# Gate slices of layer 1 loaded and stored four token tiles at a time, in place, in buffers shared with the residual

## The chip, the cores and the metric

The kernel runs on one core of a Trainium2 chip. The core has five engines with instruction streams of their own: TensorE (PE, matrix products into PSUM), VectorE (DVE), ScalarE (ACT), GpSimd (POOL) and SyncE (SP), which in this kernel issues all DMAs. The metric is the device time of one execution in microseconds; three runs of the kernel before took 1652.52, 1655.86 and 1656.51 us, a median of 1655.86.

## What is computed

Two layers over 1024 tokens of width 1024, 16 heads of 64. Layer 1 is attention with a forget gate ("fox"), layer 2 dilated sliding windows in three groups. In each, the mixer's output is multiplied by a gate and projected back onto the residual:

```python
def fox_mixer(h, w_in, b_f, q_g, k_g):
    proj = h @ w_in
    q = rms_norm(proj[..., :INNER]...)      # k, v alike
    gate = proj[..., 3 * INNER:4 * INNER]
    c = jnp.cumsum(jax.nn.log_sigmoid(f_logit), axis=1)
    o = fox_attention(q, k, v, c)           # causal softmax(q k / 8 + c_q - c_k) v
    return o.reshape(B, S, INNER), gate

x = x + (o * jax.nn.silu(gate)) @ w_out     # in each layer
```

## The kernel before

Everything is tiled by 128 tokens (8 token tiles) and by head pairs (8 pairs of 2 heads, 128 columns). A matrix product in full precision is made of three products of half-precision parts (xh, xl: high and low part of the activations; w: both parts of a weight).

Stages, in order: the gates of layer 1 (`gates`, L885 on: a projection, then silu on ACT and DVE, stored as `gs_d` in DRAM); the attention of layer 1, head pair by head pair; the output projection of layer 1 (`project_t` with `grown`, which adds the residual tile `xr`); the gates of layer 2; the attention of layer 2; the last output projection (`project_t` with `finished`, again with residual tiles `xr`).

In layer 1's attention each head pair projects queries, keys and values of one token tile after the other (`project`, L694). `heads_pair` splits queries and keys into halves `hl` and a DMA transpose brings them into `qk_t` (L843); `qs` is a copy on DVE with the halves swapped (L850). For each of the eight query tiles `fox_tile` then takes a number of steps: `score` computes the scores on PE (L870), adds the forget bias `bc` (read from `c_d` by L1088; POOL adds the mask, L1122) and takes the minimum on DVE (L1125); `p_transpose` makes the exponentials on ACT, splits them into halves `ph` (ACT and POOL, L916 and L919), and a DMA transpose on SP makes `ptt` (L920); `values` multiplies with the values on PE (L927 to L929); `finish` divides by the sum, multiplies with the gate slice and writes `y` (L1155, L1158).

The gate slice of one token tile and one head pair (128 x 128, 64 KB) is loaded in `score` (L1106) into a buffer with the tag `gsl` (3 buffers in layer 1). `finish` writes y to a tile of its own (tag `y`, 2 buffers) and stores it to `y_d` (L1162); head pair 7 does not store it, but transposes it on PE at once (`turn_last`, L729). While pair 7 runs, `turn_y` reads the stored y of the other pairs back from `y_d` (`yt`, L1178) and transposes them on PE, as input of the output projection.

The residual tiles `xr` of both output projections, the gate tiles `ge` and two small constants use the tag `n2k` (2 KB per partition) with `cfg["nb"]` buffers, 3 of them.

What the functions issue is only a list. Each step is queued for a slot of a clock (`flow`) that ticks with the projection's products. At the end `order_engines` builds a graph of all instructions (which data each needs, which buffers must come free) and `plan_engines` plays it through with a duration for each instruction: an engine takes the ready instruction whose latest start is earliest. The order found is fixed for each engine. So a change of buffers or DMAs moves instructions on every engine, as far as times in this plan shift. DMAs are all issued by SP in the planned order.

Of the kernel before, what the change touches and what calls it, by code (L numbers as in the profile page):

```python
# [11 lines left out]
F32 = mybir.dt.float32  # L12
# [5 lines left out]
ALU = mybir.AluOpType  # L18
# [4 lines left out]
P = 128  # L23
# [5 lines left out]
HD = 64  # L29
NHP = NH // 2  # L30
# [407 lines left out]
def trunk(ctx, tc, ins, out, cfg):  # L438
    nc = tc.nc
# [7 lines left out]
    def pool(name, bufs, space=None):  # L447
        kw = {} if space is None else dict(space=space)
        return book.pool(ctx.enter_context(tc.tile_pool(name=name, bufs=bufs, **kw)), name, bufs, space)
# [3 lines left out]
    sb = pool("sb", 2)  # L453
# [16 lines left out]
    def lay(shape, dtype, name, tag):  # L470
        return layer["pool"].tile(shape, dtype, name=name, tag=tag, bufs=layer["bufs"][tag])
# [3 lines left out]
    y_d = dram.tile([S, D], F32, name="y_d")  # L475
# [6 lines left out]
    gs_d = dram.tile([S, D], F32, name="gs_d")  # L482
# [372 lines left out]
    def key_runs(look):  # L855

        runs = []
        for j in look:
            if runs and j % 2 and runs[-1][0] == j - 1:
                runs[-1][1] = 2  # L860
            else:
                runs.append([j, 1])
        return runs
# [106 lines left out]
    def column_factor(t):  # L970

        sq = lay([P, D], F32, name="xsq", tag="ptt")
        nb = ps_s.tile([P, 512], F32, name="nb", tag="s")
        for h in range(2):
            nc.scalar.activation(sq[:, 512 * h : 512 * (h + 1)], xts[t, h], AF.Square)
            for k in range(4 * h, 4 * h + 4):
                nc.tensor.matmul(nb[:, :P], ones.bitcast(F32), sq[:, k * P : (k + 1) * P], start=(k == 0), stop=(k == KT - 1))
        a, y = (nb[:, i * P : (i + 1) * P] for i in (2, 3))
        r = sm.tile([P, P], F32, name="dg", tag="dg", bufs=2)
        c = sm.tile([P, P], F32, name="cf", tag="dg", bufs=2)  # L980
        nc.vector.tensor_scalar(c, nb[:, :P], 1.0 / D, EPS, ALU.mult, ALU.add)
        nc.scalar.activation(r, c, AF.Ln)
        nc.scalar.activation(r, r, AF.Exp, scale=-0.5)
        nc.scalar.activation(a, r, AF.Square)
        nc.vector.scalar_tensor_tensor(a, a, -0.5, c, ALU.mult, ALU.mult)
        nc.vector.scalar_tensor_tensor(y, a, 1.5, r, ALU.add, ALU.mult)
        return y
# [26 lines left out]
    with book.early(nc, cfg["rush"]):  # L1014
        gain_scale(0, gt)
        nb = column_factor(0)
# [5 lines left out]
    with book.early(nc, cfg["rush"] / 2):  # L1022
        nb = column_factor(1)
# [49 lines left out]
    def urgent(fn, key, slot):  # L1073
        def go():
            if cfg[key]:
                with tc.high_priority(cfg[key]):
                    fn()
            else:
                fn()

        flow.at(slot, go)
# [3 lines left out]
    def load_bc(hp, h, es=(0, 1)):  # L1085
        for e in es:
            bcs[hp, e, h] = lay([P, 5 * P], F32, name="bc", tag="ga")
            nc.sync.dma_start(bcs[hp, e, h][:, P:], c_d[2 * hp + e, h * 512 : (h + 1) * 512].partition_broadcast(P))  # L1088

    def fox_tile(hp, t, kts, vt, sl):  # L1090
        LP = cfg["lpf"]
        nk = (t + 1) * P
        st = {}
        pieces = [(a, min(a + 512, nk)) for a in range(0, nk, 512)]
        both = len(pieces) == 1
        a0 = pieces[-1][0] // P
        placed = [*range(a0), t, *range(a0, t)]
        accs = {}
        ptl = {}
        ps = {0: [], 1: []}  # L1100

        def score(e, c):
            a, b = pieces[c]
            if e == 0 and c == 0:
                gs = st["gs"] = lay([P, P], F32, name="gsf", tag="gsl")
                nc.sync.dma_start(gs, gs_d[t * P : (t + 1) * P, hp * P : (hp + 1) * P])  # L1106
            if c == 0:
                accs[e] = BIG
                st["acc"] = sm.tile([P, 2], F32, name="acc", tag="acc", bufs=8)
            if t < 2:  # L1110
                if e == 0:
                    st["p"] = lay([P, 2, nk], F32, name="p", tag="p")
                p = st["p"][:, e]
            else:
                p = lay([P, b - a], F32, name="p", tag="p")
            ps[e].append(p)
            s = ps_s.tile([P, 512], F32, name="s", tag="s")
            bc = bcs[hp, e, a // 512]
            look = key_runs(range(a // P, b // P))
            if b == nk:  # L1120
                look = [[t, 1]] + key_runs(range(a // P, t))
                nc.gpsimd.tensor_add(bc[:, :P], bc[:, b - a : b - a + P], tri)  # L1122
            scores(s, kts[t // 2], t % 2, e, [(kts[j // 2], j % 2, n) for j, n in look])
            acc = st["acc"][:, c : c + 1]
            nc.vector.tensor_tensor_reduce(p, s[:, : b - a], bc[:, : b - a] if b == nk else bc[:, P:], -1.0, accs[e], ALU.add, ALU.min, acc)  # L1125
            accs[e] = acc
            pl = (cfg["pl"] & 1, cfg["pl"] >> 1 & 1)
            if c < len(pieces) - 1 or both and e == 0:
                return
            if both:  # L1130
                exps = [(ps[i][0], accs[i]) for i in range(2)]
                if t < 2:
                    splits = [(slice(0, 2), slice(0, nk), st["p"], pl[1])]
                else:
                    splits = [(i, slice(0, nk), ps[i][0], pl[i]) for i in range(2)]
                pt = p_transpose(2, nk, exps, splits)
                for i in range(2):
                    ptl[i] = [(pt[:, i, 0, k], pt[:, i, 1, k], j) for k, j in enumerate(placed)]
            else:
                exps = [(p, accs[e]) for p in ps[e]]  # L1140
                splits = [(0, slice(*pieces[i]), ps[e][i], pl[i]) for i in range(2)]
                pt = p_transpose(1, nk, exps, splits)
                ptl[e] = [(pt[:, 0, 0, k], pt[:, 0, 1, k], j) for k, j in enumerate(placed)]

        def values(e):
            if e == 0:
                st["o"] = ps_o.tile([P, 2, HD + 1], F32, name="o", tag="o")
            pv(st["o"], e, ptl[e], vt)
            if e == 1:
                finish()  # L1150

        def finish():
            o = st["o"]
            rec = sm.tile([P, 2], F32, name="rec", tag="rec")
            nc.vector.reciprocal(rec, o[:, :, HD])  # L1155
            y = sb.tile([P, P], F32, name="y", tag="y")
            for e in range(2):
                nc.vector.scalar_tensor_tensor(y[:, e * HD : (e + 1) * HD], o[:, e, :HD], rec[:, e : e + 1], st["gs"][:, e * HD : (e + 1) * HD], ALU.mult, ALU.mult)  # L1158
            if hp == NHP - 1:
                turn_last(y, t, flow.now + 3, 0)  # L1160
            else:
                nc.sync.dma_start(y_d[t * P : (t + 1) * P, hp * P : (hp + 1) * P], y)  # L1162


        ts, tv = cfg["fox"][both]
        for e in range(2):
            for c in range(len(pieces)):
                urgent(lambda e=e, c=c: score(e, c), "ps", sl + ts[e * len(pieces) + c])
            urgent(lambda e=e: values(e), "pv", sl + LP + tv[e])
# [18 lines left out]
    def turn_last(y, t, s, layer):  # L1188
        def go():
            transpose_rows(y, KT - 1, 1, t, layer)  # L1190
            turned.add((t, 2))

        flow.at(s, go)
# [3 lines left out]
    for hp in range(NHP):  # L1197
# [11 lines left out]
        vt = v_tile(w)  # L1209
        for t in range(NT):  # L1210
            ps = project(w, tile_cols(0, t))
# [234 lines left out]
    for ci, (hp, g) in enumerate(order):  # L1446
# [5 lines left out]
        vt = v_tile(w)  # L1452
        qks = [None]
        for t in range(NT):
            if ci == NHP - 1:
                reload_x(t)
            ps = project(w, tile_cols(g, nth_tile(g, t)))
# [21 lines left out]
            else:  # L1479
                cmb = {}  # L1480
# [28 lines left out]
    layer["cm"].__exit__(None, None, None)  # L1509


CFG = dict(out={(False, 0): (), (True, 0): ((18, 20, 22, 24), (0, 0, 1, 1), 3, (4, 6, 8, 10)), (True, 1): ((18, 20, 22, 24), (14, 15, 17, 18), 24, (33, 35, 37, 39))}, take=(((33, 34, 37, 40), 42), ((62, 63, 66, 69), 71)), rush=2000, gate=(((6, 7, 8, 9), (0, 0, 1, 1), 4, (5, 6, 7, 9)), ((44, 45, 46, 47), (26, 28, 30, 32), 36, (38, 40, 42, 44)), ()), bc=((1, 0, 26), (1, 1, 28), (0, 0, 38), (0, 1, 46)), wpool=3, rbufs=8, most=(0, 2), lcm=7, ps=0, pv=100, ph_=100, ph=1, wbufs=8, pl=3, um=3, lpf=8, lsd=((16, 16), (16, 14), (14, 11)), ty2=((0, 4), (1, 5)), hb=2, ub=2, qb=1, nb=3, fox=(((0, 0, 2, 2), (2, 4)), ((0, 0), (4, 4))), due=(29, 33, 39, 45, 35, 41, 49, 57), l1=dict(ga=8, ptt=4, ph=3, p=4, qk_t=6, qs=5, vt=3, gsl=3), l2=dict(ga=4, cmb=4, gsd=4, ptt=3, ph=3, p=2, qk_t=3, og=3, vt=3, gsl=3, par=1), wload=(18, 20, 22, 24), wbound=(0, 1, 3, 4), wscale=8, wsplit=(10, 16, 22, 12))


def host_layout(inputs):
# [49 lines left out]
```

## Time and profile before

| | |
|---|---|
| median of three runs | 1655.86 us |
| the profiled execution | 1656.83 us, span 1654.8 us, granted clock 0.997 |
| gates of layer 1 | until about 122 us |
| attention of layer 1 | about 122 to 535 us |
| output projection of layer 1 | about 505 to 600 us |
| gates and attention of layer 2 | about 590 to 1600 us |
| gate loads of layer 1 | 64 of 64 KB, 138.8 to 518.9 us |
| y stores of layer 1 | 56 of 64 KB, 159.1 to 501.5 us |

In a profile row of groups or of the timeline, L1106 is a line of the kernel, "gsf<-gs_d" the tile written and the one read, and a bracket at the end names the idle time of the engine before the instruction and what ended it. "SPq" are instructions of SP that issue a DMA; their length is the time on SP, not that of the transfer. In rows by stretch, each pair of numbers is the busy time of an engine and its instruction count (PE, PE's weight loads, DVE, ACT, POOL), then PE's granted clock, the busy share of the DMA engines and GB/s. The gate slice is named `gsf` in them.

### The profile page before, as it was taken

To read this page: it belongs to the slowest core of one execution; us is meant where nothing else is said; L and a number is where in the kernel's file an instruction comes from. 1 tells how busy PE (TensorE), PEld (TensorE's weight loads), DVE (VectorE), ACT (ScalarE), POOL (GpSimd) and SP (SyncE) were. 2 spreads that over 40 slices of the span, in tenths; PEclk is the share of its full clock that TensorE was granted. 3 is DMA by queue.
4 is the path that set the end of the run, shared out by engine and by line. 5 is a ranking of instruction groups with operands and counts; after the bars stand their busy time and mean duration, and the time that the engine had idled before them with its cause. 6 is when DMAs were issued, how large, how long until landed. Compare 5 with 4: busy or idle time off the path is not lost.

```text
span 1654.8 us, 37873 instructions
## 1 busy us (share of the span) xinstructions
PE 1605.9 (97%) x13342; PEld 1037.5 (63%) x13342; DVE 1192.6 (72%) x3663; ACT 1063.5 (64%) x2746; POOL 963.9 (58%) x1252
## 2 busy tenths in 40 slices
PE   6999999999998999999999999999999999999999
PEld 4766667777664456566666666666666666666644
DVE  7757878888786586576767787777677877768751
ACT  7656778878776476566766687566566665666630
POOL 7315778778765241255555666667576766858430
PEclk9999999999999999999999999999999999999999
DMA  7335999999999884257876796768787586767952
GB/s 257 127 107 121 205 205 216 203 208 197 206 220 218 237 250 153 85 138 151 168 150 149 164 227 147 174 158 181 160 164 165 141 191 155 170 160 167 219 166 96
DMA packets 646479, 288.66 MB, mean 174 GB/s; under 512 B 493825, under 2 KB 610561, under 8 KB 646289
## 3 DMA queue, kind: packets, MB, share of 16 engines
q1 hardware_dynamic: 646288, 286.25, 74.5%
q8 instruction: 104, 1.70, 0.4%
q14 instruction: 87, 0.70, 0.1%
HBM read 124.35 MB, written 41.22 MB: 100 GB/s over the span
## 4 chain that ended last, share of the span: by engine, by line
PE 74%; DVE 10%; DMA 6%; ACT 4%; issue 3%; POOL 2%; SPq 0%; DVEq 0%; POOLq 0%; ACTq 0%
PE pj L694 56%; PE pj L719 7%; PE s L870 6%; DMA qk_t<-hl 3%; DVE w L660 2%; DVE p L1125 1%; PE ob L929 1%; PE ob L927 1%; PE ob L928 1%; DMA ptt<-ph 1%; ACT w L659 1%; PE o L929 1%; PE o L927 1%; PE o L928 1%; DVE xl L1280 1%
## 5 line engine op out<-in xcount | busy, mean ns | idle before, releaser
L694 PE MATMUL pj<-w,xh 128*128 128x384 f16 (+2 forms) x4864 | 1172.9, 324 | 6.0 <-DVE peak L904 4.3
L694 PE MATMUL pj<-w,xl 128*128 128x384 f16 (+2 forms) x2432 | 787.8, 324 | 5.2 <-DVE xl L1280 3.6
L694 PEld LDWEIGHTS <-xh 128*128 128x128 f16 x4864 | 468.1, 98 | 282.2 <-issue 8.2
L694 PEld LDWEIGHTS <-xl 128*128 128x128 f16 x2432 | 238.2, 98 | 157.5 <-DVE xl L1280 5.3
L1363 POOL TENSOR_TENSOR ph<-p,ph 128x768 f16<-128x768 f32 (+2 forms) x96 | 157.7, 1642 | 137.6 <-ACT ph L1362 130.1
L919 POOL TENSOR_TENSOR ph<-p,ph 128x512 f16<-128x512 f32 (+3 forms) x176 | 173.0, 1003 | 56.9 <-issue 37.5
L837 POOL TENSOR_TENSOR hl<-u,hl 128x512 f16<-128x512 f32 x128 | 150.9, 1179 | 53.6 <-ACT hl L836 44.9
L719 PE MATMUL pj<-xh,w 128*128 128x512 f16 x512 | 157.7, 381 | 6.2 <-DVE xr L1241 2.8
L870 PE MATMUL s<-qk_t 128*128 128x128 f16 (+1 forms) x1248 | 151.2, 238 | 6.8 <-DMA qk_t<-hl 5.1
L660 DVE SCALAR_TENSOR_TENSOR w<-raw,sws,w 128x768 f16<-128x768 f32 x96 | 146.6, 1528 | 11.0 <-ACT w L659 10.7
L794 ACT ACTIVATE sq<-pj 128x256 f32<-128x256 f32 x256 | 96.4, 377 | 86.5 <-DVE u L789 85.7
L789 DVE TENSOR_TENSOR u<-pj,gr 128x256 f32<-128x256 f32 x256 | 106.9, 418 | 45.8 <-PE pj L694 44.0
L913 ACT ACTIVATE p<-p,acc 128x512 f32<-128x512 f32 (+2 forms) x192 | 110.0, 608 | 38.0 <-DVE acc L1125 37.5
L719 PEld LDWEIGHTS <-w 128*128 128x128 f16 x768 | 74.5, 98 | 89.5 <-issue 9.2
L1352 ACT ACTIVATE p<-p,og 128x128 f32<-128x128 f32 (+1 forms) x256 | 104.1, 442 | 27.3 <-DVE og L1350 26.2
L927 PEld LDWEIGHTS <-ptt 128*128 128x128 f16 x1136 | 105.9, 98 | 19.8 <-DMA ptt<-ph 7.9
L928 PEld LDWEIGHTS <-ptt 128*128 128x128 f16 x1136 | 105.2, 96 | 11.4
L629 ACT ACTIVATE jk<-raw 128x768 f16<-128x768 f32 (+2 forms) x88 | 72.2, 820 | 62.5 <-DMA raw<-in_w_dsw 38.7
L821 POOL TENSOR_TENSOR ra<-u,cs 128x128 f32<-128x128 f32 x96 | 44.8, 467 | 108.5 <-DVE u L789 106.6
L1350 DVE CUSTOM_DVE_ANT_0 p<-s,band 128x256 f32<-128x256 f32 (+1 forms) x256 | 90.7, 373 | 22.8 <-PE s L870 22.6
L836 ACT CAST hl<-u 128x512 f16<-128x512 f32 x128 | 78.7, 614 | 42.5 <-DVE u L834 40.2
L929 PEld LDWEIGHTS <-ptt 128*128 128x128 f16 x1136 | 105.4, 97 | 0.0
(211 smaller groups left out, 3017.1 us busy)
## 6 DMA issues: line engine op xcount, KB each, us to landing
raw<-in_w_dsw SPq DMA_DIRECT2D x96, 384.0 KB, 4.2
raw<-in_w_fox SPq DMA_DIRECT2D x32, 384.0 KB, 4.1
og_d<-og SPq DMA_DIRECT2D x64, 132.0 KB, 2.5
cmb<-og_d SPq DMA_DIRECT2D x64, 132.0 KB, 2.9
bc<-c_d SPq DMA_DIRECT2D x32, 256.0 KB, 4.2
gs_d<-ge SPq DMA_DIRECT2D x32, 192.0 KB, 2.2
xt<-in_xt SPq DMA_DIRECT2D x16, 256.0 KB, 3.7
gsf<-gs_d SPq DMA_DIRECT2D x64, 64.0 KB, 2.5
```

What stands on the lines that cost most here:

```text
L660: nc.vector.scalar_tensor_tensor(w[:, 1, :, :n], raw, self.sw, w[:, 0, :, :n], ALU.mult, ALU.subtract)
L694: nc.tensor.matmul(ps[:, :n], a[:, k, cols], w.slab(k, j), start=(k == 0 and i == 0), stop=(k == KT - 1 and i == 2))
L719: nc.tensor.matmul(ps[m], ws[h].slab(k, j)[:, m * P : (m + 1) * P], a[:, k, 512 * b : 512 * (b + 1)], start=(k == 0 and x == 0), stop=(k = ...
L789: nc.vector.tensor_mul(u[:, t % 2].rearrange("p (a b) d -> p a b d", a=2), ps[:, : 4 * HD].rearrange("p (a b d) -> p a b d", a=2, b=2), gr ...
L837: nc.gpsimd.tensor_sub(hl[:, :, :4, 1], u, hl[:, :, :4, 0])
L870: nc.tensor.matmul(s[:, c0 : c0 + cnt * P].rearrange("p (c s) -> p c s", c=cnt), q, kk[:, j : j + cnt, e], start=(h == 0), stop=(h == 1), ...
L913: nc.scalar.activation(p, p, AF.Exp, bias=acc, scale=-1.0)
L919: (nc.gpsimd if pool_l else nc.vector).tensor_sub(ph[:, e, 1, cols], p, ph[:, e, 0, cols])
L927: nc.tensor.matmul(o[:, e, :], hi, vt[:, j, e, HD:], start=(b == 0), stop=False, skip_group_check=True)
L928: nc.tensor.matmul(o[:, e, :HD], hi, vt[:, j, e, :HD], start=False, stop=False, skip_group_check=True)
L929: nc.tensor.matmul(o[:, e, :], lo, vt[:, j, e, HD:], start=False, stop=(b == n - 1), skip_group_check=True)
L1363: nc.gpsimd.tensor_sub(ph[:, 1], st["p"], ph[:, 0])
```

## The change

Layer 1's gate slices are loaded for four token tiles at once (`four`: 128 partitions, 4 tiles, 128 columns; 256 KB), when the first of the four scores. The tile lies in `n2k`, which has 4 buffers instead of 3. `finish` writes y over the gate slice that it has just read. Head pairs 0 to 5 store y when the fourth tile of a group is done, in one DMA; pair 6 still stores tile by tile; pair 7 transposes each tile from the buffer. The buffers `gsl` of layer 1 and `y` are gone; `qs` gets 6 buffers instead of 5. Layer 2's own tiles stay as they were.

```diff
+    rows4 = {}
+
+    def four(d, hp, h):
+        return d.rearrange("(h j p) c -> h p j c", j=4, p=P)[h][:, :, hp * P : (hp + 1) * P]
+
     def fox_tile(hp, t, kts, vt, sl):
...
             if e == 0 and c == 0:
-                gs = st["gs"] = lay([P, P], F32, name="gsf", tag="gsl")
-                nc.sync.dma_start(gs, gs_d[t * P : (t + 1) * P, hp * P : (hp + 1) * P])
+                if (hp, t // 4) not in rows4:
+                    gs = rows4[hp, t // 4] = [sb.tile([P, 4, P], F32, name="gsf", tag="n2k", bufs=cfg["nb"]), 0]
+                    nc.sync.dma_start(gs[0], four(gs_d, hp, t // 4))
...
             nc.vector.reciprocal(rec, o[:, :, HD])
-            y = sb.tile([P, P], F32, name="y", tag="y")
+            ys = rows4[hp, t // 4]
+            y = ys[0][:, t % 4]
             for e in range(2):
-                nc.vector.scalar_tensor_tensor(y[:, e * HD : (e + 1) * HD], o[:, e, :HD], rec[:, e : e + 1], st["gs"][:, e * HD : (e + 1) * HD], ALU.mult, ALU.mult)
+                ye = y[:, e * HD : (e + 1) * HD]
+                nc.vector.scalar_tensor_tensor(ye, o[:, e, :HD], rec[:, e : e + 1], ye, ALU.mult, ALU.mult)
+            ys[1] += 1
             if hp == NHP - 1:
                 turn_last(y, t, flow.now + 3, 0)
-            else:
+            elif hp == NHP - 2:
                 nc.sync.dma_start(y_d[t * P : (t + 1) * P, hp * P : (hp + 1) * P], y)
+            elif ys[1] == 4:
+                nc.sync.dma_start(four(y_d, hp, t // 4), ys[0])
...
-CFG: nb=3, l1=dict(..., qs=5, vt=3, gsl=3)
+CFG: nb=4, l1=dict(..., qs=6, vt=3)
```

More of the change, by code (lines that the diff above doesn't have):

```diff
@@ L1509, in trunk @@
     layer["cm"].__exit__(None, None, None)
-CFG = dict(out={(False, 0): (), (True, 0): ((18, 20, 22, 24), (0, 0, 1, 1), 3, (4, 6, 8, 10)), (True, 1): ((18, 20, 22, 24), (14, 15, 17, 18), 24, (33, 35, 37, 39))}, take=(((33, 34, 37, 40), 42), ((62, 63, 66, 69), 71)), rush=2000, gate=(((6, 7, 8, 9), (0, 0, 1, 1), 4, (5, 6, 7, 9)), ((44, 45, 46, 47), (26, 28, 30, 32), 36, (38, 40, 42, 44)), ()), bc=((1, 0, 26), (1, 1, 28), (0, 0, 38), (0, 1, 46)), wpool=3, rbufs=8, most=(0, 2), lcm=7, ps=0, pv=100, ph_=100, ph=1, wbufs=8, pl=3, um=3, lpf=8, lsd=((16, 16), (16, 14), (14, 11)), ty2=((0, 4), (1, 5)), hb=2, ub=2, qb=1, nb=3, fox=(((0, 0, 2, 2), (2, 4)), ((0, 0), (4, 4))), due=(29, 33, 39, 45, 35, 41, 49, 57), l1=dict(ga=8, ptt=4, ph=3, p=4, qk_t=6, qs=5, vt=3, gsl=3), l2=dict(ga=4, cmb=4, gsd=4, ptt=3, ph=3, p=2, qk_t=3, og=3, vt=3, gsl=3, par=1), wload=(18, 20, 22, 24), wbound=(0, 1, 3, 4), wscale=8, wsplit=(10, 16, 22, 12))
+CFG = dict(out={(False, 0): (), (True, 0): ((18, 20, 22, 24), (0, 0, 1, 1), 3, (4, 6, 8, 10)), (True, 1): ((18, 20, 22, 24), (14, 15, 17, 18), 24, (33, 35, 37, 39))}, take=(((33, 34, 37, 40), 42), ((62, 63, 66, 69), 71)), rush=2000, gate=(((6, 7, 8, 9), (0, 0, 1, 1), 4, (5, 6, 7, 9)), ((44, 45, 46, 47), (26, 28, 30, 32), 36, (38, 40, 42, 44)), ()), bc=((1, 0, 26), (1, 1, 28), (0, 0, 38), (0, 1, 46)), wpool=3, rbufs=8, most=(0, 2), lcm=7, ps=0, pv=100, ph_=100, ph=1, wbufs=8, pl=3, um=3, lpf=8, lsd=((16, 16), (16, 14), (14, 11)), ty2=((0, 4), (1, 5)), hb=2, ub=2, qb=1, nb=4, fox=(((0, 0, 2, 2), (2, 4)), ((0, 0), (4, 4))), due=(29, 33, 39, 45, 35, 41, 49, 57), l1=dict(ga=8, ptt=4, ph=3, p=4, qk_t=6, qs=6, vt=3), l2=dict(ga=4, cmb=4, gsd=4, ptt=3, ph=3, p=2, qk_t=3, og=3, vt=3, gsl=3, par=1), wload=(18, 20, 22, 24), wbound=(0, 1, 3, 4), wscale=8, wsplit=(10, 16, 22, 12))
 def host_layout(inputs):
```

## The prediction

> **What bounds the kernel now.** I read the page's header first, then the busy time by stretch, then every idle stretch of TensorE (PE) in the timeline of layer 1, and last what ended those stretches in the chain and on SP.
>
> ```profile
> span 1654.8 us, 37873 instructions
> PE 1605.9 (97%) x13342; PEld 1037.5 (63%) x13342; DVE 1192.6 (72%) x3663; ACT 1063.5 (64%) x2746; POOL 963.9 (58%) x1252
> ...
> 100.00:200.00 100.00, 99.55 (x856) 65.89 (x855) 71.09 (x218) 63.62 (x164) 50.97 (x65) 1.00 0.68 155
> 200.00:300.00 100.00, 96.31 (x1049) 68.27 (x1047) 81.02 (x269) 75.37 (x187) 78.94 (x99) 1.00 1.00 205
> 300.00:400.00 100.00, 100.00 (x1109) 71.52 (x1108) 85.27 (x281) 79.24 (x197) 79.61 (x100) 1.00 1.00 204
> 400.00:500.00 100.00, 94.45 (x1009) 66.69 (x1007) 80.80 (x253) 75.89 (x182) 72.56 (x89) 1.00 1.04 211
> ...
> 500.00:505.00 5.00, 3.18 (x54) 2.53 (x55) 4.53 (x13) 3.46 (x7) 2.27 (x3) 1.00 0.96 221
> ```
>
> PE is the bound: 1605.9 of 1654.8 us. Layer 1's attention, where the changed loads and stores live, runs from about 140 to 535 us, and between 300 and 400 PE has no idle at all. A faster load there gains nothing. What the change can win in the attention is idle PE time at its two ends: 100 less the second number of each row, so 0.45 + 3.69 + 0 + 5.55, and 5.00 - 3.18 = 1.82 after 500. The sum is 11.5 us, 0.7% of the run; this is the ceiling of the gain up to 505 us.
>
> The timeline of PE names the pieces of it that count (last bracket: idle before, and who ended it):
>
> ```profile
> 226.15 0.20 PE L927 MATMUL o<-vt,ptt 128*128 128x65 f16 x1 [1.47 <-DMA ptt<-ph]
> 230.88 0.20 PE L927 MATMUL o<-vt,ptt 128*128 128x65 f16 x1 [0.77 <-DMA ptt<-ph]
> 236.13 0.20 PE L927 MATMUL o<-vt,ptt 128*128 128x65 f16 x1 [1.45 <-DMA ptt<-ph]
> ...
> 439.51 0.22 PE L870 MATMUL s<-qk_t 128*128 128x128 f16 x1 [1.04 <-DVE acc L1125]
> ...
> 501.82 0.30 PE L729 MATMUL pt<-ident,y 128*128 128x128 f32 x1 [3.16 <-DVE y L1158]
> ...
> 537.50 0.52 PE L719 MATMUL pj<-xh,w 128*128 128x512 f16 x1 [2.83 <-DVE xr L1241]
> ```
>
> The first three are one cluster: 3.69 us, transposed probabilities that land late.
>
> **What the change removes on SP.** Per head pair there were 8 gate loads and 8 stores of 64 KB. Now there are 2 loads of 256 KB, and 2 stores of 256 KB for pairs 0 to 5; pair 6 still stores by tile. In all 64 loads become 16 and 56 stores become 12 + 8, so 48 + 36 = 84 DMAs go. Bytes stay equal. The next rows give the issue time on SP (min/median/max ns) of a load and a store, what VectorE (DVE) waited for because of them, and two sizes with their landing times:
>
> ```profile
> L1106 SPq DMA_DIRECT2D gsf<-gs_d x64: 399/430/1592, 138.8 to 518.9; - x64
> L1162 SPq DMA_DIRECT2D y_d<-y x56: 320/393/1222, 159.1 to 501.5; - x56
> ...
>   DMA y_d<-y: 5.2, 6
>   DMA gsf<-gs_d: 1.4, 2
> ...
> bc<-c_d SPq DMA_DIRECT2D x32, 256.0 KB, 4.2
> gsf<-gs_d SPq DMA_DIRECT2D x64, 64.0 KB, 2.5
> ```
>
> 48 x 0.430 + 36 x 0.393 = 34.8 us of SP's issue time go, spread over 380 us. The larger DMAs that remain should cost about as much each, since bc's of 256 KB issued in 0.57 us (row at 216.92 below). DVE's 5.2 us of waiting for old y stores goes entirely, because y now lies in the gate's own place and needs no second buffer. None of this is PE time by itself. In the stretch from 255 to 400 us, nearly all of it in the head pairs where PE lost nothing, DVE waited for y stores too:
>
> ```profile
> DVE y L1158 <- DMA y_d<-y: 2.8, 3, 1.9
> ```
>
> So 2.8 of the 5.2 us cost PE nothing, and I cost the change only where PE was idle.
>
> **The cluster at 226 to 236 us.** SP's queue just ahead of it:
>
> ```profile
> 210.76 1.27 SPq L920 DMA_TRANSPOSE ptt<-ph  x1
> ...
> 215.01 0.53 SPq L1162 DMA_DIRECT2D y_d<-y  x1
> 215.64 1.23 SPq L843 DMA_TRANSPOSE qk_t<-hl  x1
> 216.92 0.57 SPq L1088 DMA_DIRECT2D bc<-c_d  x1
> 217.54 0.42 SPq L1106 DMA_DIRECT2D gsf<-gs_d  x1
> 218.01 0.43 SPq L619 DMA_DIRECT2D raw<-in_w_fox  x1
> 218.56 5.56 SPq L920 DMA_TRANSPOSE ptt<-ph  x1
> 224.16 0.58 SPq L619 DMA_DIRECT2D raw<-in_w_fox  x1
> ...
> 221.88 0.45 POOL L1122 TENSOR_TENSOR bc<-bc,band 128x128 f32<-128x128 f32 x1 [2.25 <-DMA bc<-c_d]
> ```
>
> GpSimd (POOL) waits 2.25 us for the bias row bc that SP issued only at 216.92. POOL's next step makes ph, for which the transpose at 218.56 holds SP for 5.56 us, and behind it stands the raw weight load of 224.16. A DMA on SP is late, POOL is late, SP is held, the next DMA is late. The built order shows whether the planner moves that bc. On SP, head pair 2 of layer 1 (ptt is the transpose of probabilities, qk_t of queries and keys, raw a weight load), before:
>
> ```order
> L920 DMA_TRANSPOSE ptt<-ph 128x12x128
> L1088 DMA bc<-c_d 128x512
> L920 DMA_TRANSPOSE ptt<-ph 128x12x128
> L1162 DMA y_d<-y 128x128
> L1106 DMA gsf<-gs_d 128x128
> L920 DMA_TRANSPOSE ptt<-ph 128x12x128
> L1162 DMA y_d<-y 128x128
> L843 DMA_TRANSPOSE qk_t<-hl 128x8x128
> L1088 DMA bc<-c_d 128x512
> L1106 DMA gsf<-gs_d 128x128
> L619 DMA raw<-in_w_fox 128x768
> L920 DMA_TRANSPOSE ptt<-ph 128x16x128
> ```
>
> and the same place in the changed program:
>
> ```order
> L1088 DMA bc<-c_d 128x512
> L843 DMA_TRANSPOSE qk_t<-hl 128x8x128
> L1173 DMA y_d<-gsf 128x4x128
> L920 DMA_TRANSPOSE ptt<-ph 128x10x128 x2
> L920 DMA_TRANSPOSE ptt<-ph 128x12x128 x2
> L1088 DMA bc<-c_d 128x512
> L920 DMA_TRANSPOSE ptt<-ph 128x12x128
> L843 DMA_TRANSPOSE qk_t<-hl 128x8x128
> L619 DMA raw<-in_w_fox 128x768
> L920 DMA_TRANSPOSE ptt<-ph 128x16x128
> ```
>
> The late bc (before: the second of the two, issued at 216.92) now follows directly on the second 128x12x128 transpose, ahead of the third one and of qk_t; the three small DMAs that stood ahead of it there are gone. In the trace that second transpose is the one of 210.76, off SP at 212.03. Were nothing else moved, bc would go out 216.92 - 212.03 = 4.9 us earlier, more than the 2.25 that POOL waited. That breaks the cascade at its start. But ACT and POOL have other waits there, and the order on PE, DVE and ACT is also planned anew. I take two thirds of 3.69: **-2.5 us**; the ends are -3.7 (all gone) and +3.7 (a second such cluster, the nearest row for what a bad order costs).
>
> **Head pairs 6 and 7, 400 to 505 us.** The chain that ended last passes through two of the replaced DMAs (start, length), and DVE's timeline shows the second:
>
> ```profile
> 418.94 4.43 DMA y_d<-y
> ...
> 495.52 4.79 DMA gsf<-gs_d
> ...
> 499.18 0.29 DVE L850 TENSOR_SCALAR qs<-qk_t 64x256 int32<-64x256 int32 x1 [2.28 <-DMA qk_t<-hl]
> 500.41 0.28 DVE L1158 SCALAR_TENSOR_TENSOR y<-o,rec,gsf 128x64 f32<-128x64 f32 x1 [0.94 <-DMA gsf<-gs_d]
> ```
>
> PE's 3.16 us at 501.82 is thus made of two waits of DVE in a row: 2.28 for qk_t and 0.94 for a gate tile asked for 4.79 us before. In the changed program that gate slice has been in its buffer for a long time, since its group of four was loaded for the first of them. The 0.94 goes; the qk_t wait stays and is what is late next: **-0.9 us** (ends 0 and -3.2). The y store of 418.94 delayed DVE, and 20 us later PE stood 1.04 us for DVE; other waits lie between, so I take most and not all: **-0.8 us**. The ends are -4.2 and +1.0: the stall of 3.16 began at 501.82 - 3.16 = 498.66, so 1.34 of the 5.55 belong to it and 4.2 are left to win; and one more wait of the size of the 1.04 is what a new order could cost.
>
> The one load that could be late is that of the last four tiles of pair 7. On SP, pair 7, before (xr is the output projection's residual, yt a read of y):
>
> ```order
> L1106 DMA gsf<-gs_d 128x128 x2
> L920 DMA_TRANSPOSE ptt<-ph 128x10x128 x2
> L1106 DMA gsf<-gs_d 128x128
> L1162 DMA y_d<-y 128x128
> L920 DMA_TRANSPOSE ptt<-ph 128x12x128
> L1106 DMA gsf<-gs_d 128x128 x2
> L1178 DMA yt<-y_d 128x384
> L920 DMA_TRANSPOSE ptt<-ph 128x12x128
> L1106 DMA gsf<-gs_d 128x128
> L1239 DMA xr<-in_xp 128x512 x2
> ```
>
> and after:
>
> ```order
> L920 DMA_TRANSPOSE ptt<-ph 128x10x128 x2
> L1171 DMA y_d<-gsf 128x128
> L1112 DMA gsf<-gs_d 128x4x128
> L920 DMA_TRANSPOSE ptt<-ph 128x12x128
> L1189 DMA yt<-y_d 128x384
> L920 DMA_TRANSPOSE ptt<-ph 128x12x128
> L1250 DMA xr<-in_xp 128x512 x2
> ```
>
> The group load stands right behind tile 4's own transposes (the 128x10x128 pair), where the single load for tile 4 stood one transpose later. So it costs nothing, though at 4.2 instead of 2.5 us to land it gains nothing either: 0.
>
> **The shared buffers.** Tag n2k grows from 3 to 4 buffers of 2 KB and now also serves the residual tiles of both output projections and the gate stages. In the output projection of layer 1 one of the four is held by pair 7's last group until its final transpose on PE, so three are free, as before; the 2.83 at 537.50 stays: 0. From there to about 650 us the same work is ordered a little differently, with no row that prices it: 0, with the 1.04 as end on both sides. The gate stage of layer 1 has the same order on PE, and from about 650 us on all engines have the same order too, so the last 1000 us are costed at nothing. qs with 6 buffers instead of 5 only lets the planner place a copy earlier; no row shows a wait for a qs buffer: 0.
>
> **Sum.** -2.5 - 0.9 - 0.8 = -4.2 us. The profiled execution took 1656.83 us (span 1654.8 and 2.0 around it), so 1652.6; the median of the runs is 1655.86, 0.97 lower, which makes **1651.7 us**. A measurement of this kernel can tell about 0.3%, 5.0 us, from no change, so 1651.7 lies just inside "no change" and the border is at 1650.9.
>
> **Rivals.** First, *all the idle goes*: SP's relief of 34.8 us clears every stall up to 505 us, 11.5 us, giving 1655.86 - 11.5 = 1644.4. For it speaks that SP carries every transpose in one queue; against it, that some rows end in a DVE wait for DVE or ACT work, and the qk_t wait is not touched. Chance 0.15.
>
> Second, *nothing*: SP is held less by issuing than by data:
>
> ```profile
> SPq L920 <- POOL ph L919: 68.7, 41, 4.9
> ```
>
> SP waited 68.7 us in 41 waits for POOL's ph before a transpose. Time saved ahead of such a wait only makes the wait longer, PE's stalls stay, and the time is 1655.5. The Trainium skill, "DMA: Bandwidth & Descriptors", section "Issuing engines are not separate DMA queues", has a rule on this side: what is saved by shortening the issue is usually small relative to the DMA itself. By that rule alone the result would be this rival's; the trace agrees for one load (0.43 of 2.5 us), and only the cascade at 218 us speaks against it. Chance 0.23.
>
> Third, *slower*: a 256 KB load directly ahead of a transpose delays it. In the new order a ptt transpose stands right behind each group load. A 256 KB DMA lands 4.2 - 2.5 = 1.7 us later than a 64 KB one; if the transpose behind it loses as much where PE already waits for ptt (three rows above, and again at pair 7 and at one fresh place), that is 5 x 1.7 = 8.5 us, 1664. It decides from the point where the transpose behind a group load is the last thing PE waits for. Against it: bc's 256 KB loads stand ahead of transposes already, and the same pattern ran at 100% PE between 300 and 400. The same page, section "Queues, rings and completion order", says that each DMA engine takes descriptors in the ring's order, which is this mechanism; no run here shows its price. Chance 0.10.
>
> **Numbers.** My own case has 0.52; its own range is 1648 to 1655. Faster by over 0.3%: 0.15 from the first rival and 0.25 from my case, 0.40. Within 0.3%: 0.27 and 0.23, 0.50. Slower: 0.10. The range of 1646 to 1658 leaves out the third rival and about half of the first.
>
> **What would show it.** Right: no PE stall on ptt between 220 and 240; no DVE wait for y_d or gsf in the profile after; about 84 fewer DMA issues; the 3.16 at 501.82 smaller by about a microsecond; PE still without idle time between 300 and 400; the stretch from 700 us to the end unchanged in length. Wrong: stalls on ptt in each head pair right behind a group load, or a new stall where the cluster was, or a gain that lies in the output projection or layer 2.

## The result, and the profile after

The changed kernel takes 1646.37 us (median of 7 runs, 1642.33 to 1648.67) against 1655.86: a ratio of 0.9948 with a 95% interval of 0.9930 to 0.9965. That is faster by 0.52% (8.6 us) by the ratio, and by 9.5 us between the medians. The forecast was 1651.7, a gain of 4.2 us. The result lies in the range of 1646 to 1658, but only 0.4 us above its lower end, and it is faster by more than 0.3%, to which the forecast had given a chance of 0.40, against 0.50 for no change. The profiled execution took 1647.55 us, and its span is 9.0 us shorter than before.

The page after, its first lines: PE is still the bound. Over the whole run 4.6 of the 9.0 us are busy time of PE and 4.4 are idle time; inside the attention, where the change is, nearly all is idle time.

```profile
span 1645.8 us, 37723 instructions
...
PE 1601.3 (97%) x13342; PEld 1035.8 (63%) x13342; DVE 1204.2 (73%) x3663; ACT 1061.6 (65%) x2746; POOL 962.9 (59%) x1252
```

Busy time by stretch, after (the second number of a row is PE's busy time, 100.00 or 5.00 is all of it):

```profile
200.00:300.00 100.00, 100.00 (x1095) 71.56 (x1093) 87.11 (x282) 78.32 (x199) 81.15 (x103) 1.00 1.01 208
300.00:400.00 100.00, 100.00 (x1114) 71.63 (x1112) 85.55 (x275) 79.85 (x195) 82.01 (x98) 1.00 0.97 203
400.00:500.00 100.00, 96.21 (x1053) 68.25 (x1050) 86.55 (x265) 76.49 (x184) 72.57 (x90) 1.00 1.07 220
500.00:505.00 5.00, 5.00 (x64) 3.59 (x63) 4.41 (x13) 4.22 (x9) 4.57 (x5) 1.00 0.54 162
```

From 200 to 400 us PE never stops. The 3.69 us before 300 are gone, and so are the 1.82 after 500; of the 5.55 between 400 and 500, 3.79 are left. The gain can be followed by instructions that do the same work in both programs. The last y of pair 7 is transposed at 531.81 us before and at 524.43 after, 7.4 us earlier: most of the 9.0 us is gained by the end of the attention of layer 1. From its first score (141.55 us before, 141.10 after) to this transpose the attention is 6.9 us shorter, of which 6.3 are idle time of PE and 0.6 busy time. The other busy time went elsewhere: 2.5 us in the gates of layer 1, where PE idles 2.1 us longer instead, and 1.5 us behind the attention, where the trace before has a stretch at half clock that the one after lacks (599.04 to 602.45; the last section tells more of these).

What is left of PE's waits at its end (timeline of PE, after):

```profile
451.20 0.29 PE L870 MATMUL s<-qk_t,qs 128*128 128x128 f16 x2 [0.91 <-DVE qs L850]
...
522.65 0.20 PE L927 MATMUL o<-vt,ptt 128*128 128x65 f16 x1 [1.47 <-DMA ptt<-ph]
524.43 0.30 PE L729 MATMUL pt<-ident,gsf 128*128 128x128 f32 x1 [0.86 <-DVE gsf L1166]
...
530.12 0.38 PE L719 MATMUL pj<-xh,w 128*128 128x512 f16 x1 [1.22 <-DVE xr L1252]
```

The 3.16 us that stood before the transpose of a y at 501.82 have no successor. They hung on DVE, whose waits for qk_t between 140 and 540 us were, before,

```profile
DVE qs L850 <- DMA qk_t<-hl: 7.8, 7, 2.3
```

(us in total, times, longest), and are after, with the largest new one beside it,

```profile
DVE xr L1252 <- DMA xr<-in_xp: 5.8, 1, 5.8
...
DVE qs L850 <- DMA qk_t<-hl: 2.7, 3, 1.6
```

Nothing is left in that list for an old y store or a gate load. The DMA issues of SP (min, median and longest ns):

```profile
L1112 SPq DMA_DIRECT2D gsf<-gs_d x16: 432/540/1232, 138.3 to 493.9; - x16
L1173 SPq DMA_DIRECT2D y_d<-gsf x12: 370/444/542, 186.0 to 429.4; - x12
L1171 SPq DMA_DIRECT2D y_d<-gsf x8: 382/471/578, 434.2 to 493.4; - x8
```

16 + 12 + 8 = 36 DMAs in place of 64 + 56 = 120: the 84 that should go are gone. One of 256 KB costs SP little more than one of 64 KB did (medians of 540 for 430 ns for a load, and 444 for 393 for a store).

### The profile page after: what moved, and what is told of

Read it like the earlier page. It is cut to its first block, busy times and chain, and to the rows that moved or that the text cites. A ratio compares the mean times of both kernels' runs of the same rounds, so it can differ in the third digit from the quotient of the medians.

```text
span 1645.8 us, 37723 instructions
## 1 busy us (share of the span) xinstructions
PE 1601.3 (97%) x13342; PEld 1035.8 (63%) x13342; DVE 1204.2 (73%) x3663; ACT 1061.6 (65%) x2746; POOL 962.9 (59%) x1252
## 4 chain that ended last, share of the span: by engine, by line
PE 79%; DVE 8%; DMA 5%; ACT 3%; issue 3%; POOL 1%; SPq 0%; DVEq 0%; POOLq 0%; ACTq 0%
PE pj L694 60%; PE pj L719 7%; PE s L870 7%; DMA qk_t<-hl 3%; DVE w L660 2%; PE ob L929 1%; PE ob L927 1%; PE o L929 1%; PE ob L928 1%; PE o L927 1%; DMA ptt<-ph 1%; PE o L928 1%; DVE xs L1286 1%; ACT w L659 1%; DVE xl L1291 1%
## 5 line engine op out<-in xcount | busy, mean ns | idle before, releaser
L660 DVE SCALAR_TENSOR_TENSOR w<-raw,sws,w 128x768 f16<-128x768 f32 x96 | 150.9, 1574 | 9.5 <-ACT w L659 9.2
L928 PEld LDWEIGHTS <-ptt 128*128 128x128 f16 x1136 | 105.3, 96 | 11.5
```

Of the source, the lines that this page charges most:

```text
L660: nc.vector.scalar_tensor_tensor(w[:, 1, :, :n], raw, self.sw, w[:, 0, :, :n], ALU.mult, ALU.subtract)
L928: nc.tensor.matmul(o[:, e, :HD], hi, vt[:, j, e, :HD], start=False, stop=False, skip_group_check=True)
```

## The experiments

Three theories stood at the start. **A** (A1 where it is told apart from other effects of larger transfers): it is the number of DMAs on SP's one queue; each that goes lets every transpose behind it start earlier, and PE waits less all along the attention. **B**: it is the drawn order; any edit makes the planner lay out all engines anew, this draw was a good one, and the 84 DMAs have little to do with it. **C**: it is the buffers; y in the gate's place no longer waits for one of two y buffers. Ratios below are to the kernel before in the same job (median 1655.57 to 1656.02 us there), with 95% intervals.

**1. The group as four transfers, ordered by the planner.** The change's buffers, but 64 + 56 DMAs of 64 KB, all four loads of a group issued at its first tile:

```diff
-                    nc.sync.dma_start(gs[0], four(gs_d, hp, t // 4))
+                    for j in range(4):
+                        nc.sync.dma_start(gs[0][:, j], four(gs_d, hp, t // 4)[:, j])
...
-                nc.sync.dma_start(four(y_d, hp, t // 4), ys[0])
+                for j in range(4):
+                    nc.sync.dma_start(four(y_d, hp, t // 4)[:, j], ys[0][:, j])
```

> The changed kernel's buffers and its places in time, but each load and each store of four tiles is issued as four DMAs of 64 KB, one behind the other (64 loads, 48 + 8 stores). Theory A, SP's queue: the gain of 8.6 us (ratio 0.9948) comes from the 84 DMAs that SP no longer issues; here all 84 are back, so most of the gain is lost, 1653 to 1656. Theory B, a lucky plan: any new order lands somewhere within 4 us of 1651, so between 1647 and 1655 and without relation to the count. Theory C, y's two buffers: y still lies in place and waits for no store, so the gain stays, 1646 to 1648.

1660.67 us, 1.0034 (1.0021 to 1.0047): the whole gain is gone, and more, above the range of every theory. The direction fits A, but the planner made a new order, so B isn't out.

**2 to 4. One half of the grouping, or none.** In 2 the loads are grouped and every pair stores by tile; in 3 each tile loads its own slice of the shared tile and the stores are grouped; 4 has both edits, so only the change's buffers and the writing in place are left.

```diff
-            elif hp == NHP - 2:
+            else:
                 nc.sync.dma_start(y_d[t * P : (t + 1) * P, hp * P : (hp + 1) * P], y)
-            elif ys[1] == 4:
-                nc.sync.dma_start(four(y_d, hp, t // 4), ys[0])
```

```diff
...
-                    nc.sync.dma_start(gs[0], four(gs_d, hp, t // 4))
+                nc.sync.dma_start(rows4[hp, t // 4][0][:, t % 4], gs_d[t * P : (t + 1) * P, hp * P : (hp + 1) * P])
```

> Loads of four tiles as in the changed kernel, every y stored by its tile (16 loads, 56 stores). Theory A: 48 of the 84 DMAs stay away, 48/84 of 8.6 is 4.9 us, so 1651. Theory B: 1647 to 1655 without relation to the count. Theory C: 1646 to 1648.

> Stores of four tiles as in the changed kernel, every gate slice loaded by its tile into its place in the shared tile (64 loads, 20 stores). Theory A: 36 of the 84 DMAs stay away, 3.7 us, so 1652. Theory B: 1647 to 1655 without relation to the count. Theory C: 1646 to 1648.

> Only the buffers of the change: y over the gate slice, in shared tiles of four with 4 buffers, but every slice loaded and every y stored by its tile (64 loads, 56 stores as before). Theory A: no gain, 1655 to 1657. Theory B: 1647 to 1655. Theory C: the whole gain, 1646 to 1648, and no wait of VectorE for a y store in the profile.

| ratio (interval) | 56 stores | 20 stores |
|---|---|---|
| 64 loads | 1.0054 (1.0034 to 1.0074), 1663.90 us | 0.9987 (0.9976 to 0.9999), 1653.95 us |
| 16 loads | 1.0006 (0.9992 to 1.0020), 1655.75 us | 0.9948 (0.9930 to 0.9965), the change |

Grouping the loads gives 0.48% (upper row to lower, left) or 0.39% (right); grouping the stores 0.67% or 0.58%. The two nearly add. But the left column also holds lost clock: in their traces PE ran at half clock for three stretches in 4 and for one in 2, 5.1 and 1.7 us lost (last section). The buffers and the writing in place alone give no gain, though 4 has no wait of DVE for a y store any more; this speaks against C. The order of the four fits A; its numbers were missed by 2 (1651 expected) and by 4 (1655 to 1657). B would need four draws that happen to fall in this pattern, which these alone don't exclude.

**5 to 7. The order drawn again.** `SLACK` (L128) is the margin in ns that the plan adds to waits between engines. Another value changes no instruction, only the order, and that from the gates of layer 1 on (PE's order differs first at about 42 us with 160). 160 was tried for the kernel before (5), the change (6) and the kernel of experiment 4 (7).

```diff
-SLACK = 150
+SLACK = 160
```

> The kernel before, only with the planner's constant SLACK at 160 instead of 150, so that the same instructions and DMAs stand in another order from the attention on. Theory A (the number of DMAs on SP sets the time, the order hardly matters): 1654 to 1658, as before. Theory B (any new order draws the time anew): anywhere between 1648 and 1664, more than 3 us away from 1655.6 as likely as not.

> The changed kernel, only with SLACK at 160 instead of 150. Theory A: 1645 to 1649, as the changed kernel, and clearly below the kernel before with SLACK 160. Theory B: the gain of 8.6 us was the draw of one order, and this draw falls between 1646 and 1662.

> The change's buffers with every DMA as before (64 loads, 56 stores), with SLACK at 160 instead of 150. With 150 it took 1663.9. Theory A: the loss of 8 us against the kernel before belongs to the buffers, so it stays, 1662 to 1666. Theory B: it was the draw of an order with three long stalls, and the time comes back to 1653 to 1659.

Before: 1658.68 us, 1.0017 (1.0000 to 1.0033). After: 1654.48, 0.9991 (0.9975 to 1.0006). In place only: 1658.49, 1.0008 (0.9990 to 1.0026). The draw alone moved the changed kernel by 0.43%, almost as much as the gain, and experiment 4's kernel by 0.46%. A's range of 1645 to 1649 for the changed kernel was missed. So B has a real part: with this margin the change is worth 0.26% (about 0.03 to 0.49), not 0.52%. And the grouping alone, in-place kernel against changed kernel, is worth 0.17% there, with about 0.24 of uncertainty on each side, where it was 1.07% with a margin of 150: in this order its worth is not clear of zero.

**8. A third y buffer in the kernel before**, which takes away no DMA:

```diff
-            y = sb.tile([P, P], F32, name="y", tag="y")
+            y = sb.tile([P, P], F32, name="y", tag="y", bufs=3)
```

> The kernel before with 3 buffers for y instead of 2, so that VectorE waits less for old y stores (5.2 us in 6 waits before); all DMAs as before. Theory A: these waits were hidden, 1654 to 1657. Theory C (y's buffers carry the gain): 1647 to 1651. Theory B: 1648 to 1664.

1661.33 us, 1.0032 (1.0015 to 1.0049), no gain, and outside the ranges of A and C. It says little of C: DVE still waited 4.0 us for old y stores (5.2 before), and the order is a new draw.

**9. The number of DMAs alone, at the changed kernel's own order.** The decisive run. The planner sees each 256 KB group as one step, so the order on every engine is the change's to the instruction (the traces bear it out); then four DMAs of 64 KB are issued in that one place.

```diff
-                    nc.sync.dma_start(gs[0], four(gs_d, hp, t // 4))
+                    with book.glue(nc):
+                        for j in range(4):
+                            nc.sync.dma_start(gs[0][:, j], four(gs_d, hp, t // 4)[:, j])
...
+    def glue(self, nc):
+        n = len(nc.cur_bb.bb.instructions)
+        yield
+        first, *rest = list(nc.cur_bb.bb.instructions)[n:]
+        self.glued[first.name] = rest
...
+        line = [j for i in line for j in (i, *book.glued.get(i.name, ()))]
```

(The store likewise.)

> The changed kernel with its very own order on every engine, but each 256 KB load and store issued as four DMAs of 64 KB in direct succession (84 more on SP, 28 places). Theory A1 (SP's issue time is what the change saves): 84 more DMAs at 0.4 us each are 34 us on SP, most of the gain of 8.6 us is lost, 1652 to 1656. Theory B (the order alone carries the gain): 1645 to 1649, as the changed kernel. The same split with a plan of its own took 1660.7.

1659.33 us, 1.0022 (1.0006 to 1.0038). Against the change that is 1.0022 / 0.9948, so +0.74%, some 12 us, for nothing but 84 more DMAs; adding the half-widths of the two ratios in squares gives about 0.5 to 1.0%. Experiment 10, the change again in all but a buffer, ran in the same job as this one: 1659.33 / 1646.78 is +0.76%. And against the kernel before, which has the same 120 DMAs, the change's order and buffers alone are slower by 0.22%. So with this order the gain doesn't come from the order: it is -0.74% for the DMAs and +0.22% for the rest. C falls here as well: the buffers are the change's, DVE waits for no y store, and there is no gain. The expectation of A1, 1652 to 1656, was too low.

The traces show the way. PE's busy time in the 400 us of the attention, first before, then after, then experiment 9:

```profile
140.00:540.00 400.00, 383.42 (x4093) 267.94 (x4092) 319.65 (x1026) 301.32 (x728) 295.23 (x362) 1.00 0.98 203
```

```profile
140.00:540.00 400.00, 391.35 (x4129) 271.68 (x4128) 328.91 (x1026) 302.01 (x731) 297.60 (x364) 1.00 0.98 207
```

```profile
140.00:540.00 400.00, 382.45 (x4088) 266.93 (x4087) 324.96 (x1023) 298.93 (x725) 292.83 (x361) 1.00 0.94 202
```

PE stands 16.58, 8.65 and 17.55 us. The four transfers in place of one bring all the idle time back. The DMA engines were not fuller for it: their share (the number before the last) is 0.94, against 0.98. What differs is SP's queue. Added up from its timeline, the time between 140 and 530 us that no DMA row covers is 56.5 us before, 100.5 after and 74.0 in experiment 9. So the queue isn't full on the whole, but there are stretches in which it is. One of them, in pair 3, of experiment 9:

```profile
275.62 1.39 SPq L852 DMA_TRANSPOSE qk_t<-hl  x1
277.06 0.57 SPq L1097 DMA_DIRECT2D bc<-c_d  x1
277.73 2.64 SPq L1186 DMA_DIRECT2D y_d<-gsf  x4
280.42 0.42 SPq L1097 DMA_DIRECT2D bc<-c_d  x1
280.90 1.84 SPq L1123 DMA_DIRECT2D gsf<-gs_d  x4
282.85 2.04 SPq L929 DMA_TRANSPOSE ptt<-ph  x1
285.00 1.31 SPq L852 DMA_TRANSPOSE qk_t<-hl  x1
286.40 3.58 SPq L929 DMA_TRANSPOSE ptt<-ph  x2
290.04 1.99 SPq L1123 DMA_DIRECT2D gsf<-gs_d  x4
292.14 1.66 SPq L929 DMA_TRANSPOSE ptt<-ph  x1
```

and of the changed kernel, the same instructions:

```profile
272.45 1.70 SPq L843 DMA_TRANSPOSE qk_t<-hl  x1
274.20 0.57 SPq L1088 DMA_DIRECT2D bc<-c_d  x1
274.86 0.38 SPq L1173 DMA_DIRECT2D y_d<-gsf  x1
275.30 0.49 SPq L1088 DMA_DIRECT2D bc<-c_d  x1
275.84 0.45 SPq L1112 DMA_DIRECT2D gsf<-gs_d  x1
278.25 3.32 SPq L920 DMA_TRANSPOSE ptt<-ph  x1
281.68 1.25 SPq L843 DMA_TRANSPOSE qk_t<-hl  x1
283.02 3.12 SPq L920 DMA_TRANSPOSE ptt<-ph  x2
286.20 0.57 SPq L1112 DMA_DIRECT2D gsf<-gs_d  x1
286.87 1.25 SPq L920 DMA_TRANSPOSE ptt<-ph  x1
```

In experiment 9 a row starts within 0.11 us of the end of the one before it: SP is never free, and from the first qk_t transpose to the start of the last ptt transpose it takes 292.14 - 275.62 = 16.52 us. In the changed kernel the same way takes 14.42 us, with 1.96 us in it in which SP is free (276.29 to 278.25). The length of a row also holds waiting for data: in the changed kernel SP comes to the first ptt transpose 3.3 us sooner after the qk_t transpose, and then waits 5.2 us there for POOL's ph, up to the end of the row of 3.32 us. So of the 3.3 us saved on issuing, 2.1 come through. PE pays in both kinds of transpose (timeline of PE, experiment 9):

```profile
288.06 0.20 PE L936 MATMUL o<-vt,ptt 128*128 128x65 f16 x1 [1.41 <-DMA ptt<-ph]
...
457.88 0.40 PE L879 MATMUL s<-qk_t 128*128 128x128 f16 x3 [1.82 <-DMA qk_t<-hl]
```

What isn't told apart is why a DMA costs SP's queue this much: the time on SP itself (the four of a group take 1.84 to 2.64 us, one 0.38 to 0.57), or also something that each transfer costs behind the queue. Nor is it shown that the DMAs are worth as much in another order.

**10. Five qs buffers instead of six.**

```diff
-CFG: l1=dict(..., qs=6, vt=3)
+CFG: l1=dict(..., qs=5, vt=3)
```

> The changed kernel with 5 buffers for qs, as before, instead of 6. Theory A: qs has no part in it, 1645 to 1649. Theory B: a new order, a new draw, 1646 to 1660.

1646.78 us, 0.9953 (0.9937 to 0.9968): the same as the change. The sixth buffer has no part (the order on PE and DVE is the same with five), and the result has been measured a second time.

**11 and 12. A third order for both kernels**, `SLACK = 140`, the edit of experiment 5 with another number.

> The changed kernel with the planner's SLACK at 140, a third order of the same instructions (150: 1646.4, 160: 1654.5). If the change has a gain of its own beside the draw, it lies below the kernel before with SLACK 140 by some 4 to 8 us; if the draw is all, the two don't differ in a steady direction.

> The kernel before with SLACK at 140, a third order of the same instructions (150: 1655.9, 160: 1658.7). A gain of the change beside the draw: this lies at 1652 to 1660, 4 to 8 us above the changed kernel with SLACK 140. Draw alone: 1647 to 1664.

After: 1651.74 us, 0.9984 (0.9970 to 0.9997). Before: 1665.89, 1.0073 (1.0051 to 1.0095). Over three draws of the order (margins of 140, 150 and 160) the change is worth 0.88% (0.9984 / 1.0073), 0.52% and 0.26%, 0.55% on average, each time a gain; but the draws of one kernel lie up to 0.73% (before) and 0.43% (after) apart. No version here is faster than the changed kernel.

## Why the prediction was right, and where not

**The bound and the place: right.** PE is the bound, and most of the gain is idle PE time in layer 1's attention. Of the 11.5 us of idle between 140 and 505 us, 0.85 (140 to 200) + 3.79 = 4.64 are left, so 6.9 went, where the sum had 4.2. The signs of being right that it named came out, the 3.16 us by more than it said: no stall on ptt between 220 and 240, no DVE wait for an old store or a gate load, 84 fewer DMAs, no idle PE between 300 and 400, and from one and the same instruction, at 701.17 before and 692.93 after, the rest of the run lasts 953.6 and 952.9 us.

**The cluster, -2.5: right, and too small.** All 3.69 went. The cascade was cut where the prediction cut it, as SP's timeline after shows:

```profile
202.70 7.84 SPq L920 DMA_TRANSPOSE ptt<-ph  x3
210.60 0.57 SPq L1088 DMA_DIRECT2D bc<-c_d  x1
211.37 1.41 SPq L920 DMA_TRANSPOSE ptt<-ph  x1
212.90 1.83 SPq L843 DMA_TRANSPOSE qk_t<-hl  x1
```

bc goes out at 210.60 instead of 216.92, ahead of the third transpose and of qk_t, and POOL has no wait for bc there any more. Taking two thirds for fear of other waits cost 1.2 us. The cause is the order, as the prediction had it: in experiment 9, with the same order and all 84 DMAs back, bc goes out ahead of the third transpose too (212.28 us), and of the 3.69 us no more than 0.88 stand between 200 and 255.

**The 3.16 us, -0.9: the step that failed.** The prediction said that the gate wait goes but "the qk_t wait stays and is what is late next". All of it went: the third transpose of a y of pair 7, at 501.82 before, comes at 490.94 after, without a wait of PE. That is 2.3 us of the shortfall, the largest piece. With the 84 DMAs back in the same order it doesn't return: in experiment 9 this transpose comes at 504.19, again without a wait (one of 0.94 us for another DMA, yt, ends just ahead of it). What the DMAs do set is how late the transposes of queries and keys are in all, since these stand in the same queue: DVE's waits for qk_t are 7.8 us before, 2.7 after, and in experiment 9

```profile
DVE qs L859 <- DMA qk_t<-hl: 8.8, 11, 1.4
```

So the prediction treated a wait that isn't named after a removed DMA as one that stays, and neither the new order nor the shorter queue left it there.

**What the sum of stalls leaves out.** Experiment 9 has the new order, the gate slices in place and no wait for an old y store, so all that the three terms of the prediction go by, and the two large stalls are gone from it. Yet it is not faster than the kernel before: PE's idle time stands at other places instead, such as the 1.41 us at 288.06 and the 1.82 at 457.88. What the missing DMAs give is that these new stalls don't arise. So the prediction named the places of the gain rightly, but what it gave as their reasons gives no gain taken alone; it needs the relief of SP, which the prediction took for no PE time by itself.

**The 1.04 us, -0.8: half of it.** Between 400 and 500 us 5.55 - 3.79 = 1.76 went, of which 1.34 belong to the 3.16; so 0.4 is left for this term, since new waits such as the 0.91 at 451.20 took its place. The stretch before also holds waits of PE of 0.96 (at 461.98) and 1.22 us (at 471.64, for a qs copy), which the prediction doesn't list. Between 140 and 200 PE idles 0.4 more than before (0.85 for 0.45). The four give -3.7 - 3.2 - 0.4 + 0.4 = -6.9.

**The xr stall, 0: it did change.** 2.83 became 1.22; the ptt wait just ahead of it grew from 0.74 (at 530.03) to 1.47. Why it shrank is not shown; in experiment 9 it is 2.83 again. Over the stretch from 140 to 540 as a whole, PE's idle time fell by 7.9.

**Layer 2, 0: not contradicted.** From the xr stall to the last one (1599.18 before, 1589.47 after) it is 1061.7 us before and 1059.4 after. Lost clock is more than this difference: in that part the trace before has two stretches at half clock (from 537.60 and 599.04, 1.7 us lost each) and the one after has none. Experiment 9, with the change's own order there and one such stretch (from 540.69), has 1601.86 - 541.00 = 1060.9.

**Rivals.** "All the idle goes" gave 1644.4 and was nearest, though 4.64 us of the idle stayed. "Slower" didn't come: a transpose stands behind each group load, and PE didn't wait from 200 to 400. "Nothing" was half right in its mechanism. SP's waits for POOL before a ptt transpose, between 140 and 530 us, after:

```profile
SPq L920 <- POOL bc L1128: 68.7, 41, 5.2
SPq L920 <- POOL ph L919: 56.5, 27, 5.2
```

The row that goes with the 68.7 us for ph shown of before is

```profile
SPq L920 <- POOL bc L1122: 30.5, 26, 3.2
```

so 99.2 us became 125.2. All rows of that view added up are 172.1 us before, 224.9 after and 194.8 in experiment 9: of the time that 84 DMAs less save on SP at a fixed order, some 30 us turned into longer waits, as that rival said. Its error was to take that for all. Where SP has no gap, a saved DMA is a transpose that starts earlier. The rule that it took from the Trainium skill ("DMA: Bandwidth & Descriptors", section "Issuing engines are not separate DMA queues": the time to initiate a DMA is usually small relative to the DMA itself) is about one transfer, and each single issue here is small, 0.43 of 2.5 us. Experiment 9 decides against using it for the sum: 84 of them cost some 12 us.

**The size, and luck.** A gain of 9 us for 34.8 us less issue time could not be summed from four stalls of one trace, because the stalls that the missing DMAs prevent are not in that trace. Nor is its exact size the change's own: another draw of the order gave 0.26%, a third 0.88%. That the result fell into the range, 0.4 us from its end, is thus in part the luck of the draw; with the margin of 160 the same change gives 4.2 us between the medians, the very gain of the forecast, and with 140 it gives 14. That the count of DMAs makes the gain is shown for the order at hand (9); the table of 2 to 4 fits it, the pair of experiments 6 and 7 leaves it open for their order. That the order decides whether it is 4 or 14 us is shown as well (5, 6, 11, 12).

## What to carry to other kernels

When one queue issues both small loads and the transposes that the critical engine waits for, look for stretches in which the queue has no gap: there a DMA that goes can let everything behind it start earlier, also what bears another name. Don't price such a change by the waits that name the removed DMA. The idle time of the critical engine in the stages concerned bounds what can be won there (11.5 us here, of which 6.9 went); how much of it goes could not be told from the waits of one trace. And where a planner draws the order anew at each edit, compare several draws of both versions, or hold the order fixed and change the suspected cost alone, before a half per cent is put down to the edit.

## What was not expected of the hardware

PE's granted clock fell to half for 3.41 us at a time after waits that were not long. In experiment 4, PE idled 2.30 us before

```profile
226.35 0.50 PE L694 MATMUL pj<-w,xh 128*128 128x384 f16 x2 [2.30 <-DVE u L834]
```

and the busy time in steps of 3.41 us (the clock is the third number from the end) shows

```profile
223.70:227.11 3.41, 1.11 (x8) 0.51 (x6) 3.41 (x9) 2.79 (x9) 3.41 (x4) 1.00 0.97 328
227.11:230.52 3.41, 3.41 (x37) 2.75 (x35) 2.77 (x5) 1.93 (x5) 1.79 (x2) 0.50 1.01 215
230.52:233.94 3.42, 3.42 (x29) 2.38 (x27) 3.27 (x11) 2.81 (x7) 0.00 (x0) 1.00 1.43 259
```

Two more waits of that run, of 2.46 and 1.94 us (ending at 329.14 and 461.95), did the same, from 329.51 and 462.62 on. Each time half of 3.41 us is 1.7 us of clock lost, 5.1 in all, in which PE counts as busy. That goes some way to explain why this kernel took 1663.90 us while its PE idled less between 140 and 540 us than that of the kernel before (14.3 us against 16.58). Yet the kernel before kept its full clock through the wait of 3.16 us at 501.82. The Trainium skill, "TensorE: Matmul & The Clock Gate", section "HAM oscillation — how this bites in real kernels", gives the rule that PE should have no idle gaps above about 3.4 us. Here gaps of 1.94 to 2.46 us were enough and one of 3.16 was not, so the length of the gap alone doesn't decide.

The traces show what does. The stretches at half clock of one run begin on a fixed grid: from 227.11 to 329.51 it is 102.40 us, 30 steps of 3.413, and from there to 462.62 it is 133.11, 39 steps. Each of the three waits lies inside one step. The wait of 3.16 us lies across a border of its run's grid (500.05 is 11 steps ahead of the half clock that begins at 537.60):

```profile
496.64:500.05 3.41, 2.02 (x11) 0.92 (x10) 0.52 (x3) 2.08 (x5) 2.66 (x4) 1.00 1.37 93
500.05:503.46 3.41, 1.64 (x33) 1.49 (x34) 2.99 (x9) 1.93 (x5) 0.73 (x2) 1.00 0.94 216
503.46:506.88 3.42, 3.42 (x51) 2.50 (x49) 3.42 (x10) 3.32 (x7) 3.25 (x3) 1.00 0.78 195
```

That makes 1.39 and 1.77 us of idle time in two steps, and the clock stays. So what counts is PE's idle time within one step. In all 14 traces, from 45 us on and leaving out steps already at half clock, each of the 29 steps with 1.96 us of idle time or more was followed by half clock, of 13 steps with 1.90 to 1.96 one was, and of some 6500 with less one (1.79 us). A wait of 2 to 3 us therefore costs 1.7 us of clock or nothing, by where it falls on the grid.
